# The delta-rule walk emitted in half steps, each tied to its place on TensorE

## The chip, the cores and the metric

The kernel runs on one core of one Trainium2 chip. The metric is the device time of one execution in microseconds; 2858.76 us is the median of three runs of the kernel before. A profile was taken of one further execution.

## The reference, cut to what matters

Two layers of a decoder, each with four mixers side by side on one input projection: HGRN2 (A), gated delta rule (B), Mamba-2 SSD (C), retention (D). The prompt has 2048 positions behind 16 learned ones, so 2064 rows of width 1024; eight sample sequences of one token come along. Each mixer has four heads of 64 x 64 state. The change concerns the gated delta rule, which passes a state S from chunk to chunk:

```
def chunk_gated_delta(S, xs):
    ...
    sol = lax.linalg.triangular_solve(lhs, rhs, left_side=True, lower=True, unit_diagonal=True)
    u = sol[..., :dv] - jnp.einsum('bhik,bhkv->bhiv', sol[..., dv:], S)
    qk = jnp.einsum('bhik,bhjk->bhij', q, k) * decay
    o = (jnp.einsum('bhik,bhkv->bhiv', q * jnp.exp(G)[..., None], S)
         + jnp.einsum('bhij,bhjv->bhiv', qk, u))
    S_new = (jnp.exp(g_last)[..., None] * S
             + jnp.einsum('bhjk,bhjv->bhkv', k * jnp.exp(g_last - G)[..., None], u))
```

The u of a chunk needs the state, and the state of the next chunk needs u: a chain.

## The kernel before, in words

**Stages.** A layer runs the mixers one after the other: C, then B's dense part and preparation, then A (HGRN), then D (retention), then the output projection. The 2064 rows are 17 tiles: tile 0 with 32 prompt rows (and the 8 samples), tiles 1 to 16 with 128 rows. Tiles are dealt to 8 blocks of two (the first has three). A dense group (`dense_cm`, L484 to L486) is 24 matmuls on one PSUM buffer "pd" of two, with one eviction behind it; `dense_rows` (L494 to L496) is the same by rows.

**The walk.** The delta rule's chain is worked in chunks of 32 tokens, so a tile has 4 steps and tile 0 has one. The chain can't be done in one go without leaving TensorE idle, so it is a Python generator, `walkB`, that runs along with the dense part of B and with A: wherever the code calls `hook()`, the generator is advanced to its next `yield` and emits a piece of the walk there. In B's dense part a hook stands after each dense group (8 a block); in A a block of two tiles has 6 hooks between its dense groups and 9 in its inner part (one after the first score level, a double one after each of two further levels, one after each of two last levels, one after each of two tiles), and the first block has 5 more for tile 0. What is left after D would be emitted in one go before the output projection.

**One step** (`stepB`, L1253 to L1273) does, in this order: two state products on TensorE (`wo<-sbd,bnq`, L236), VectorE's add that makes the step's u (`wz<-bwi,wo`, L1264), a copy of it on GpSimd (`bwi<-wz`, L244), the update product on TensorE (`tr<-wz,bkt`, L236, in a PSUM buffer "tr" of two that all mixers share), ScalarE's decay of the old state (`low`, L306), VectorE's two adds that make the new state (`sbd<-low,tr`, L313), and ScalarE's copy of the step's output rows (`boq<-wo`, L1273). Each fp32 product of two halves shows as four matmuls in the trace. The next step's state products need the new state.

**A tile** begins with `loadB` of the next tile (two loads, `bld<-qkv` and `bld<-bscu`, and two smaller ones, on SP's queue; the second of each group's first tile goes on GpSimd's). After the second to fourth step one of three pieces of `keysB` is emitted, which prepares the next tile (transposes of keys and values L1212 and L1213, decay factors, products with the solved inverse). At its end the 32 x 32 score products (`wo<-bwi,bma`) are written to the walk's own PSUM buffer, the one that held the state products ("wo", one buffer), and VectorE adds them to the output (L1331); then `finish` starts the group normalisation, and its rest (two transposes, two VectorE operations, the store) is emitted after the next tile's first step.

**What sets the order.** The instructions are emitted in the order of the Python code, with priorities in that order (`early()` raises some); a scheduler then orders each engine's queue by priority among those that its own estimate takes to be ready. `inorder((ET.PE,))` ties the TensorE instructions emitted inside it behind the last TensorE instruction emitted before it. Before the change only the pieces of `keysB` in a tile are tied so (KORD is 1), the steps, the scores and `finish` are not. Constants in use: LAG 3 (yields after a first load), KB0 1 (keys from the second step on).

Weights, activations, the walk's loads and other tiles share pools: "f4" has five buffers for weight pieces `wr`, the walk's `bld` and A's and the output projection's rows. The weights of A are loaded while the last blocks of B's dense part run.

## Time and profile before

| | |
|---|---|
| runs of the kernel before | 2858.45, 2858.76, 2864.55 us; median 2858.76 |
| profiled execution, its own time | 2864.64 us |
| its span, first to last instruction | 2862.9 us |
| mean granted TensorE clock | 0.982 of full speed |
| instructions | 66636 |

PE is TensorE's matmuls, PEld its weight loads, DVE VectorE, ACT ScalarE, POOL GpSimd, SP the engine whose queue issues most DMAs. Names such as `wz<-bwi,wo` say which tile is written from which. In a timeline a row is a run of like instructions: start, duration, engine, line, operation, tiles, shapes, count, and in brackets the idle time of the engine before it and what ended it.

### The profile page before, as it was taken

How to read it: one execution, taken by the hardware profiler on the slowest of the kernel's cores; microseconds unless marked ns; L12 is line 12 of the kernel's file. 1: busy time of each engine (PE TensorE's matmuls, PEld its weight loads, DVE VectorE, ACT ScalarE, POOL GpSimd, SP SyncE). 2: the span in 40 equal slices, each digit the busy share in tenths (PEclk: the TensorE clock that was granted, in tenths of full speed). 3: DMA queues.
4: the chain of work that ended last, by engine and by line, in shares of the span. 5: the costliest groups of instructions: out<-in, count | busy, mean ns of one | idle time of the engine just before them, and what ended most of it. 6: DMA issues, size and time to landing. Idle time of an engine off the chain costs nothing.

```text
span 2862.9 us, 66636 instructions
## 1 busy us (share of the span) xinstructions
PE 2713.3 (95%) x26372; PEld 2463.7 (86%) x26372; DVE 1704.0 (60%) x4864; ACT 1034.1 (36%) x2601; POOL 1065.6 (37%) x2032
## 2 busy tenths in 40 slices
PE   6999999989999899999989999999999999999998
PEld 6889898989889788888778999888898887888787
DVE  5777765657656655454346767656676667445533
ACT  4545532333434422232244445223443443222321
POOL 4454545557323221110033535555773322211100
PEclk9999999999999999999999999999999999999999
DMA  7243445563321423236672433544632323331443
GB/s 179 67 142 110 147 128 139 149 173 102 98 74 61 150 77 113 77 112 204 211 231 80 127 108 119 141 121 134 184 82 90 88 83 114 98 108 67 139 140 111
DMA packets 385152, 349.31 MB, mean 122 GB/s; under 512 B 144312, under 2 KB 349616, under 8 KB 374600
## 3 DMA queue, kind: packets, MB, share of 16 engines
q1 hardware_dynamic: 381320, 335.95, 38.8%
q0 software_dynamic: 3520, 9.09, 1.7%
q8 instruction: 209, 3.42, 0.5%
q14 instruction: 103, 0.84, 0.1%
HBM read 247.05 MB, written 98.10 MB: 121 GB/s over the span
## 4 chain that ended last, share of the span: by engine, by line
PE 74%; DVE 8%; DMA 7%; POOL 4%; ACT 3%; issue 3%; SPq 1%; POOLq 0%; ACTq 0%; DVEq 0%
PE pd L494 10%; PE pd L496 9%; PE pd L495 9%; PE pd L484 9%; PE pd L485 8%; PE pd L486 8%; PE tr L236 7%; PE wo L236 4%; PE sc L236 4%; PE o L236 3%; DMA wr<-in_w_in_dram 3%; PE tr L622 1%; ACT wh L458 1%; PE tr L518 1%; POOL bR L1168 1%
## 5 line engine op out<-in xcount | busy, mean ns | idle before, releaser
L484 PE MATMUL pd<-xh,wh 128*128 128x256 f32 (+1 forms) x2816 | 828.4, 294 | 34.7 <-DVE hB L959 11.5
L486 PE MATMUL pd<-xh,wl 128*128 128x256 f32 (+1 forms) x2816 | 814.8, 289 | 0.6 <-DVE wl L459 0.6
L485 PE MATMUL pd<-xl,wh 128*128 128x256 f32 (+1 forms) x2816 | 815.3, 290 | 0.0
L484 PEld LDWEIGHTS pd<-xh,wh 128*128 128x128 f32 x2816 | 542.7, 193 | 56.9 <-issue 20.0
L494 PE MATMUL pd<-wh,xh 128*128 128x512 f32 (+5 forms) x1632 | 563.1, 346 | 7.4 <-DVE sraw L1406 4.4
L495 PE MATMUL pd<-wl,xh 128*128 128x512 f32 (+5 forms) x1632 | 558.2, 342 | 5.1 <-POOL wl L459 4.4
L496 PE MATMUL pd<-wh,xl 128*128 128x512 f32 (+5 forms) x1632 | 558.2, 342 | 0.0
L486 PEld LDWEIGHTS pd<-xh,wl 128*128 128x128 f32 x2816 | 542.8, 193 | 5.2 <-issue 3.2
L485 PEld LDWEIGHTS pd<-xl,wh 128*128 128x128 f32 x2816 | 542.9, 193 | 3.1 <-issue 1.3
L494 PEld LDWEIGHTS pd<-wh,xh 128*128 128x128 f32 (+1 forms) x1632 | 304.1, 186 | 45.7 <-issue 4.6
L495 PEld LDWEIGHTS pd<-wl,xh 128*128 128x128 f32 (+1 forms) x1632 | 304.4, 187 | 41.6 <-POOL wl L459 5.0
L496 PEld LDWEIGHTS pd<-wh,xl 128*128 128x128 f32 (+1 forms) x1632 | 304.0, 186 | 38.6 <-issue 1.7
L313 DVE TENSOR_TENSOR sbd<-low,tr 64x128 f32<-64x128 f32 x384 | 109.0, 284 | 130.0 <-PE tr L236 116.1
L336 POOL TENSOR_TENSOR fm<-fm,expo 128x4 f32<-128x4 f32 (+3 forms) x136 | 131.1, 964 | 80.0 <-DVE fm L613 72.6
L611 POOL TENSOR_SCALAR fm<-fm 128x4 f32<-128x4 f32 (+3 forms) x102 | 25.0, 245 | 352.1 <-DVE fm L608 325.4
L340 POOL TENSOR_SCALAR rm<-rm 128x1 f32<-128x1 f32 (+1 forms) x51 | 14.0, 275 | 353.5 <-ACT junk L358 352.5
L244 POOL COPY bwi<-wz 32x256 f32<-32x256 f32 x128 | 59.8, 467 | 206.7 <-DVE wz L1264 203.7
L531 ACT ACTIVATE th<-pd 128x256 f32<-128x256 f32 (+2 forms) x162 | 62.5, 386 | 187.4 <-PE pd L486 143.5
L1168 POOL TENSOR_TENSOR bR<-bR,bW 128x120 f32<-128x120 f32 (+14 forms) x300 | 119.0, 397 | 21.0
L1167 POOL TENSOR_TENSOR bW<-bU,bR 128x120 f32<-128x120 f32 (+14 forms) x300 | 112.8, 376 | 33.2 <-DMA bR<-bscr 12.8
L1674 DVE TENSOR_TENSOR hx<-hx,pd 128x512 f32<-128x512 f32 (+1 forms) x68 | 46.6, 686 | 119.9 <-PE pd L496 118.5
L513 DVE SCALAR_TENSOR_TENSOR hx<-hx,rm,sq 128x512 f32<-128x512 f32 (+1 forms) x68 | 53.1, 819 | 104.5 <-POOL rm L336 103.5
(531 smaller groups left out, 5135.6 us busy)
## 6 DMA issues: line engine op xcount, KB each, us to landing
xh<-xh SPq DMA_DIRECT2D x56, 1024.0 KB
xl<-xl SPq DMA_DIRECT2D x56, 1024.0 KB
wr<-in_w_in_dram SPq DMA_DIRECT2D x64, 512.0 KB
hx<-in_x_prompt_dram SPq DMA_DIRECT2D x32, 512.0 KB
y<-y SPq DMA_DIRECT2D x128, 128.0 KB
yf<-y SPq DMA_DIRECT2D x32, 512.0 KB
bld<-qkv SPq DMA_DIRECT2D x32, 384.0 KB
xh<-xh SPq DMA_DIRECT2D x8, 1184.0 KB
```

The costliest lines, as they stand in the source:

```text
L236: T.matmul(out, l, r, start=start, stop=stop, skip_group_check=True)
L313: tt(new[rr, :, hh], low[rr, :, hh], pv, ALU.add)
L336: G.tensor_tensor(dst, src, e.broadcast_to(list(src.shape)), ALU.pow)
L484: T.matmul(ps, hi[:, d], b.xh[:, d, 0:b.n], start=(d == 0), stop=False)
L485: T.matmul(ps, hi[:, d], b.xl[:, d, 0:b.n], start=False, stop=False)
L486: T.matmul(ps, lo[:, d], b.xh[:, d, 0:b.n], start=False, stop=(d == 7))
L494: T.matmul(ps[0:R, 0:n], xh[:, d], hi, start=(d == 0), stop=False)
L495: T.matmul(ps[0:R, 0:n], xh[:, d], lo, start=False, stop=False)
L496: T.matmul(ps[0:R, 0:n], xl[:, d], hi, start=False, stop=(d == 7))
L531: act(th[0:R, 0:n], ps, AF.Tanh, scale=0.5)
L1167: f(wv, bcm(U_[0:2 * nu, j, j + 1:32], 1, m), bcl(R_[0:2 * nu, 0:m, j], 31 - j), ALU.mult)
L1168: f(R_[0:2 * nu, 0:m, j + 1:32], R_[0:2 * nu, 0:m, j + 1:32], wv, ALU.subtract)
```

## The change

`stepB` gets a `yield` between the state products (with VectorE's add and the copy) and the update. In `walkB` each half is emitted at a hook of its own, and all that is emitted at a hook is tied on TensorE behind what was emitted before. With each half comes one other piece at most: first the ended tile's remainder (two pieces, the scores with the normalisation, then the transposes and the store), else a load that is missing, else, from the second step on, a piece of the next tile's keys. The scores go to a "tr" buffer. The turn of its own that a tile's end, its rest and each piece of keys had is gone.

```diff
--- before.py
+++ after.py
@@ -1265,6 +1265,7 @@
             gcopy(wt[r], xw_[r])
         else:
             V.tensor_copy(xw_[r], wt[r])
+        yield
         R = 128 if SB is not None else 32
         pu = update(lambda p: X.kt[0:R, 2 * p:2 * p + 2].rearrange("t h k -> t (h k)"), xw_[0:R])
         next_state(L, "B", pu, lambda p: X.eg[:, p, 32 * bb + 31:32 * bb + 32])
@@ -1290,8 +1291,20 @@
             x = next(src, 0)
             return x and loadB(L, *x)
 
-        Z = Y = None
-        last = None
+        def ends(X):
+
+            def scores():
+                pi = ptile(ptr, "tr")
+                blocks32(lambda r, h: pi[r, 64 * h:64 * h + 64], X.ma, X.wi.rearrange("t (h v) -> t h v", h=4), X.Lc, True)
+                if X.t == 0:
+                    V.tensor_copy(L.o0[0:32], pi[0:32, 0:256])
+                    L.z0 = dec_z(X.z)
+                    return None
+                tt(X.oq, X.oq, pi[:, 0:256], ALU.add)
+                return finish(X.t, 1, X.oq, 128, X.P.epsq[:, X.i], L.wB, X.z)
+            return scores
+
+        Z = last = None
         done = 0
         while done < NT:
             X = Z
@@ -1307,32 +1320,25 @@
             X.wo = ptile(pwo, "wo")
             X.oq = bk([128, 256], "boq")
             for bb in range(X.Lc // 32):
-                stepB(L, X, bb)
-                yield
-                if last:
-                    last()
-                    last = None
+                step = stepB(L, X, bb)
+                for half in range(2):
+                    with inorder((ET.PE,)):
+
+                        next(step, 0)
+                        if last:
+                            last = last()
+                        elif not Z:
+                            Z = load()
+                        elif bb >= KB0 or X.t == 0:
+                            if not hasattr(Z, "keys"):
+                                Z.keys = keysB(L, Z)
+                            next(Z.keys, 0)
                     yield
-                if not Z:
-                    Z = load()
-                elif bb >= KB0:
-                    if not hasattr(Z, "keys"):
-                        Z.keys = keysB(L, Z)
-                    with inorder((ET.PE,)) if KORD else ExitStack():
-                        k = next(Z.keys, 0)
-                    if k != 0:
-                        yield
-            pi = X.wo
-            blocks32(lambda r, h: pi[r, 64 * h:64 * h + 64], X.ma, X.wi.rearrange("t (h v) -> t h v", h=4), X.Lc, True)
-            if X.t == 0:
-                V.tensor_copy(L.o0[0:32], pi[0:32, 0:256])
-                L.z0 = dec_z(X.z)
-            else:
-                tt(X.oq, X.oq, pi[:, 0:256], ALU.add)
-                last = finish(X.t, 1, X.oq, 128, X.P.epsq[:, X.i], L.wB, X.z)
+            last = ends(X)
             done += 1
+        while last:
+            last = last()
             yield
-        last()
         store_state(L.S["B"], o["gdn_p"][L.l])
 
     def decB(L, ys, epsq):
```

## Rows read from the trace of the kernel before

**Rows 1.** The page, part 1: busy us (share of the span) and instructions of each engine

```profile
PE 2713.3 (95%) x26372; PEld 2463.7 (86%) x26372; DVE 1704.0 (60%) x4864; ACT 1034.1 (36%) x2601; POOL 1065.6 (37%) x2032
```

**Rows 2.** Busy time by stretch: columns in the first line

```profile
core 0: us, PE busy (x) PEld busy (x) DVE busy (x) ACT busy (x) POOL busy (x), PEclk, DMA share, GB/s
455.00:627.00 172.00, 159.38 (x2009) 151.02 (x1998) 97.59 (x294) 60.49 (x144) 92.96 (x199) 0.96 0.54 154
627.00:1022.00 395.00, 376.65 (x5151) 341.99 (x5149) 264.14 (x861) 156.94 (x430) 162.07 (x391) 0.98 0.31 92
1880.00:2035.00 155.00, 147.87 (x1821) 139.71 (x1822) 91.97 (x278) 54.06 (x135) 83.56 (x177) 0.97 0.51 147
2035.00:2432.00 397.00, 379.62 (x5164) 344.17 (x5163) 267.10 (x860) 159.85 (x432) 170.33 (x408) 0.99 0.33 98
```

**Rows 3.** Timeline, TensorE in the delta-rule stage: start us, duration us, what

```profile
500.34 0.61 PE L236 MATMUL tr<-wz,bkt 128*128 128x128 f32 x4
...
503.75 0.61 PE L236 MATMUL wo<-sbd,bnq 128*128 128x128 f32 x4
```

**Rows 4.** Busy time by stretch, four short stretches, columns as in rows 2

```profile
830.50:842.50 12.00, 7.11 (x38) 5.61 (x34) 6.54 (x20) 5.18 (x16) 4.49 (x8) 0.72 0.35 97
...
633.00:662.00 29.00, 29.00 (x301) 27.37 (x301) 17.61 (x74) 8.29 (x25) 21.29 (x48) 1.00 0.46 124
...
2244.00:2256.00 12.00, 8.36 (x51) 6.77 (x52) 7.31 (x23) 5.28 (x16) 4.19 (x8) 0.72 0.35 95
...
594.00:616.00 22.00, 12.96 (x87) 12.34 (x87) 8.40 (x20) 7.94 (x14) 10.67 (x15) 0.77 0.91 211
```

**Rows 5.** Timeline, TensorE in an HGRN block's inner part; idle time before in brackets

```profile
832.37 0.71 PE L236 MATMUL tr<-wz,bkt 128*128 128x128 f32 x4 [1.15 <-DVE wz L1264]
...
833.92 0.68 PE L236 MATMUL wo<-sbd,bnq 128*128 128x128 f32 x4 [0.38 <-DVE sbd L313]
...
835.77 1.22 PE L236 MATMUL tr<-wz,bkt 128*128 128x128 f32 x4 [1.17 <-DVE wz L1264]
...
839.19 1.19 PE L236 MATMUL wo<-sbd,bnq 128*128 128x128 f32 x4 [1.78 <-DVE sbd L313]
```

**Rows 6.** Waits of TensorE, whole span: total us, times, longest us

```profile
PE tr L236 <- DVE wz L1264: 7.2, 10, 1.2
...
PE wo L236 <- DVE sbd L313: 6.1, 8, 1.8
...
PE tr L1212 <- DMA bld<-qkv: 3.8, 3, 1.8
...
PE tr L236 <- DVE sbd L313: 2.8, 6, 0.7
```

**Rows 7.** Instructions on the tile bwi: ns min/median/max, first and last start us

```profile
L236 PE MATMUL wo<-bwi,bma x1040: 214/214/239, 463.1 to 2428.0; 32*32 32x64 f32 x174
```

**Rows 8.** Busy time on tile wz alone, HGRN stage: PE, PEld, DVE, POOL

```profile
627.00:1022.00 395.00, 34.15 (x200) 27.69 (x200) 20.45 (x49) 23.40 (x49) 0.98 0.31 92
```

**Rows 9.** Waits of TensorE in the HGRN stages, layer 0 and layer 1

```profile
PE sc L236 <- DVE ak L795: 2.2, 1, 2.2
...
PE sc L236 <- ACT sq L841: 2.6, 3, 1.5
```

**Rows 10.** Timeline: a first-of-group load on SP, and its transposes on TensorE

```profile
528.01 1.72 SPq L1188 DMA_DIRECT2D bld<-qkv  x2
...
534.03 0.33 PE L1212 MATMUL tr<-ident,bld 128*128 128x128 f32 x1 [1.81 <-DMA bld<-qkv]
```

**Rows 11.** Timeline of SP and VectorE near 600 us; TensorE's wait behind it

```profile
594.30 4.22 SPq L1190 DMA_DIRECT2D bld<-bscu  x1
...
602.50 6.26 SPq L451 DMA_DIRECT2D wr<-in_w_in_dram  x3
...
599.70 1.22 DVE L459 TENSOR_TENSOR wl<-wr,wh 128x1024 fp32r<-128x1024 f32 x1 [6.35 <-ACT wh L458]
...
PE pd L484 <- DVE hB L959: 6.3, 1, 6.3
```


## Prediction

> **What bounds the kernel now.** I read the page's busy line first, then busy time by stage, then who TensorE waits for, then single stretches of the timeline. TensorE has a matmul in flight for 95% of the span and VectorE works 60% [rows 1]: it is a matmul kernel with 2862.9 - 2713.3 = 149.6 us of matmul idle time. By stage [rows 2]: the delta-rule walk (the chain of 32-token steps) begins in the delta-rule stage and ends in the HGRN stage of each layer. From its first step on, the rest of the delta-rule stage (455 to 627, 1880 to 2035) has 12.6 and 7.1 us of matmul idle time, the HGRN stage (627 to 1022, 2035 to 2432) 18.4 and 17.4. So the change works on 55.5 us of idle time, plus what the granted clock (0.96 to 0.99 there) takes.
>
> Where does the walk itself stop TensorE? Beside dense groups, not at all: an update starts at 500.34 and the next state product at 503.75 [rows 3], 3.41 us apart with a dense group of 24 matmuls between them, and 633 to 662 has 29.00 us of matmuls in 29 us [rows 4]. Here each half of a step already has its dense group. In the inner part of an HGRN block the dense groups run out, and steps stand one behind the other: TensorE waits 1.15 us for the update, 0.38 for the next product, 1.17 for the update, 1.78 for the product [rows 5]. That stretch of 12 us has 7.11 us of matmuls and a granted clock of 0.72, as its twin in layer 1 has (8.36 us, 0.72) [rows 4]. Over the whole span the walk's handoffs cost TensorE 7.2 us (update waiting for VectorE's add) and 6.1 us (product waiting for the new state); 2.8 us go to "tr" work waiting for VectorE's state adds, mostly for one of the two PSUM buffers that they hold [rows 6].
>
> **The change, part by part.** I sum against the profiled execution's own time, 2864.64 us (span 2862.9), which is 5.9 above the median of the runs, 2858.76; the same difference is then applied to the median.
>
> **1. Fewer turns.** A turn is one advance of the walk by a hook. Counting yields, a full tile takes 9 turns now (4 steps, 1 for the last tile's rest, 3 for keys, 1 for the tile's end) and 8 then; a layer's walk 151 now and 139 then (3 after the first load, 3 for its keys, 2, 1, 16 x 8, 2 at the end). The delta-rule stage gives 40 turns (5 blocks of 8), the HGRN stage 125 (20, then 7 x 15). So the walk's emission ends at HGRN turn 111 of 125 now and 99 then: 12/15 of a block, some 40 us earlier at (1022 - 627)/8 = 49 us a block [rows 2]. No operation is added or taken away. VectorE, 264.14 busy of 395 us there, covers the denser walk; were that cover gone, 0.83 more steps a block at about 1 us of VectorE would cost 0.8 us a block, 11 us in 14 blocks. I take 0: the last block gets it back.
>
> **2. Halves apart.** The handoffs cost 7.2 + 6.1 + 2.8 = 16.1 us [rows 6]; they lie in HGRN's inner parts. Of a block's 15 turns, 6 follow dense groups and 9 lie in the inner part; 4 of these 9 come as two double turns, where the two halves (or an update and the next product) still stand together. Ends: 0 (each wait only moves) and -16.1. I take the five ninths that get the block's own work in between: **-8.9**. The clock of the two thin stretches costs (1 - 0.72) x 12 = 3.4 us each [rows 4]; ends 0 and -6.7, and the same share gives **-3.7**.
>
> **3. The tile's end.** The 1040 small score matmuls [rows 7] move behind the next tile's first product and from the walk's own PSUM buffer to the shared pair "tr". The walk then takes 9 "tr" buffers a tile instead of 8. A wait of that kind is 2.8/6 = 0.47 us long; ends 0 and 32 tiles x 0.47 = +15. Most find a buffer free, so I take an eighth of 2.8, **+0.4**. The normalisation behind it (ScalarE, VectorE, GpSimd, then two transposes and the store on SP's queue) moves by one turn with the same instructions: 0, since nothing before the output projection reads the store; SP has it in its order either way.
>
> **4. TensorE's order is tied.** Each half's matmuls now come behind the last matmul emitted before them, in the inner part one of HGRN's own, which may itself wait for VectorE or ScalarE. Until now only the keys were tied so; products, updates, scores and transposes could go ahead and fill such a wait. Queued behind a tied half are the next block's dense groups, which are emitted later and may be scheduled ahead of it. Bounds: nothing if those fill instead; at most, with 200/4 = 50 updates a layer in that stage [rows 8], 2 x 50 x 2 halves x 9/15 = 120 halves of 0.61 us of matmuls [rows 3] = +73. The nearest rows are HGRN's own score waits, 2.2 and 2.6 us [rows 9], small today; I let them double: **+4.8**.
>
> **5. Keys and loads.** The next tile's load is issued as now, at a tile's start, but its keys come after 2 turns instead of 3. This counts only for the first tile of a group, the only one not loaded long before: its load was issued at 528.01 and its transposes waited 1.81 us until 534.03 [rows 10]; both layers 3.8 us [rows 6]. Two turns are 2 x 3.41 = 6.8 us, the landing took about 6: I take 0, ends -3.8 and +6.8 (a turn's 3.41 in each layer). The load's four issues (three on SP, and one on SP or GpSimd's queue) move with the tile's start past SP's weight and activation loads. One such place is costly now: the scheduler put load issues among HGRN's weight loads (4.22 us and then 6.26 us on SP), and a dense group waited 6.3 us for VectorE, which stood behind a late weight [rows 11]; the 22 us around it have 12.96 us of matmuls at a clock of 0.77 [rows 4], so 9.0 + 5.1 = 14 us. Layer 1 has no such stall. I take 0, with -14 and +14 as its ends.
>
> **Sum:** -8.9 - 3.7 + 0.4 + 4.8 = **-7.4 us**: 2857.2 for the profiled execution, **2851.4** for the median (-0.26%). A measurement of this kernel can tell about 0.2%, 5.7 us, from no change.
>
> **The rivals.**
> *Nothing measurable.* Beside dense groups the schedule already has the order that the change writes down [rows 3], and in the inner part a wait only goes from one handoff to another. For: VectorE and TensorE take turns there, whoever is served first. Against: the thin stretches are runs of whole steps, which the change breaks up. 2858.8, give or take 4.
>
> *Slower: the walk no longer fills.* If HGRN's own matmuls wait in the inner part and the tied halves stand behind them, TensorE idles where it did a half. From 12.6/0.61 = 21 of the 120 halves on this eats the gain; at 40 it is +24.4 - 12.6 + 0.4 = +12: 2871. For: when the update waited 1.17 us, TensorE did nothing else [rows 5]. Against: HGRN's own waits are short now, and later dense groups may fill. The Trainium skill (TensorE: Matmul & The Clock Gate, step 1 of Part 2) says that only weight loads are pulled ahead and matmuls stay in program order. That speaks against this change, which fixes more of the order, and the trace agrees at that wait. A weight stall as in part 5 arising in layer 1 as well would end near here too, 2851.4 + 14 = 2865.
>
> *Faster by more.* Weight loads filled 27.37 of 29 us, 94%, at full matmul pace [rows 4]; in the two HGRN stretches they fill 686.2 of 792 us [rows 2], so these would take 686.2/0.944 = 727 us at that pace: a room of 65 us where matmul idle time shows 35.8. If half of the room is the walk's, -32: 2826; if the weight stall alone goes, 2837. For: the thin stretches come at block ends. Against: the small matmuls there never run at dense pace. The Trainium skill (Perfetto Trace Analysis, Identifying the Most-Contended Engine) holds matmul busy time for a bad measure of room and weight-load time for a good one. By that rule the larger room is the real one; no row here settles it.
>
> **How the numbers follow.** Small gain as summed (2844 to 2858): 0.36. Nothing measurable: 0.26. Slower: 0.24. Larger gain: 0.14. Faster by over 0.2% (below 2853.0) takes the larger gain and 0.30 of the small one, 0.44; within, 0.26 + 0.06 = 0.32; slower (above 2864.5) 0.24. Faster and slower cases together hold most of the chance; the likeliest one's own range is 2844 to 2858. The range for 8 in 10, 2834 to 2873, reaches to the stall's -14 on one side and to the +12 rival on the other; it leaves out deeper cases of either kind.
>
> **What would show it.** Part 1: the walk's last step in layer 0 some 40 us earlier than now. Part 2: TensorE's waits for the add and the new state fall from 13.3 to under 8 us, and no 12 us stretch at 0.72 in the HGRN stages. Part 3: "tr" waits on state adds still near 3 us. Part 4: HGRN's score waits near 10 us in both layers together; over 20 means the slower rival. Part 5: first-of-group transposes wait 2 us or less. If idle time between 627 and 1022 doesn't fall, the sum is wrong whatever the time.

## The result, and the profile after

The changed kernel takes **2896.13 us** (median of four runs, 2892.57 to 2913.57), the kernel before 2858.61 beside it: a ratio of **1.0142** (95% interval 1.0118 to 1.0166). It is slower by 1.4%, where -0.26% was forecast; the range of 2834 to 2873 missed it by 23 us. The profiled execution took 2898.79 us with a span of 2897.1, so 34.2 us more than the span of before. One execution of the run below with GpSimd tied took 6029.27 us, about twice the others, for no reason that the record shows; without it that run's median is 0.2 us lower.

The page of the changed kernel, part 1:

```profile
PE 2729.6 (94%) x26372; PEld 2474.9 (85%) x26372; DVE 1702.2 (59%) x4864; ACT 1033.9 (36%) x2601; POOL 1053.6 (36%) x2032
```

Every engine has as many instructions as in [rows 1]. Matmul idle time is 2897.1 - 2729.6 = 167.5 us, 17.9 more than before, and the same 26372 matmuls are in flight 16.3 us longer, at a mean granted clock of 0.978 instead of 0.982. So about half of the loss is waiting and half is matmuls that take longer, and no line of the page says where.

To place it, I marked points of equal TensorE work in both traces (each matmul counted by its usual spacing) and compared the time between them. The busy time of the changed kernel by stretch; columns as in [rows 2], whose stretch of layer 0's HGRN stage comes first; then the stretches between points of equal work, and three short ones:

```profile
627.00:1022.00 395.00, 366.90 (x4965) 330.82 (x4964) 249.37 (x824) 152.70 (x418) 155.82 (x386) 0.96 0.32 92
...
617.00:1033.50 416.50, 388.19 (x5176) 349.09 (x5175) 263.98 (x870) 161.20 (x434) 165.56 (x408) 0.96 0.32 94
...
1033.50:1922.60 889.10, 856.32 (x6589) 774.74 (x6588) 502.49 (x1312) 303.90 (x744) 291.59 (x466) 0.99 0.45 135
1922.60:2054.90 132.30, 117.48 (x1413) 112.40 (x1412) 75.72 (x225) 41.48 (x101) 59.84 (x117) 0.94 0.56 155
2054.90:2464.60 409.70, 382.81 (x5185) 345.51 (x5185) 262.79 (x862) 161.06 (x435) 164.25 (x407) 0.97 0.31 92
2464.60:2897.10 432.50, 423.22 (x2550) 362.98 (x2548) 189.33 (x418) 102.28 (x211) 63.24 (x120) 1.00 0.33 109
...
594.00:616.00 22.00, 19.12 (x262) 17.80 (x260) 9.82 (x27) 8.51 (x17) 10.30 (x16) 1.00 1.03 257
850.00:866.00 16.00, 11.99 (x162) 9.58 (x160) 8.53 (x24) 5.61 (x17) 5.95 (x13) 0.79 0.45 129
2026.00:2052.00 26.00, 13.09 (x147) 12.33 (x137) 7.80 (x14) 6.30 (x10) 8.97 (x13) 0.74 0.94 233
```

The same points of work in the kernel before:

```profile
625.00:1014.10 389.10, 370.87 (x5026) 337.13 (x5025) 256.53 (x834) 157.35 (x429) 161.32 (x391) 0.98 0.32 93
...
1014.10:1914.40 900.30, 866.72 (x6738) 781.76 (x6737) 506.15 (x1340) 304.42 (x745) 292.82 (x467) 0.98 0.45 134
1914.40:2033.90 119.50, 112.92 (x1421) 108.17 (x1420) 74.68 (x230) 43.13 (x107) 60.39 (x118) 0.99 0.57 159
2033.90:2423.40 389.50, 372.12 (x5025) 337.68 (x5025) 259.93 (x832) 158.67 (x430) 168.61 (x404) 0.99 0.34 100
2423.40:2862.90 439.50, 427.52 (x2711) 366.00 (x2709) 198.63 (x450) 103.45 (x215) 66.36 (x124) 1.00 0.33 108
```

Read the second column of both, length by length. Up to the first point (617 against 625) the changed kernel is 8.0 us ahead; HGRN costs it 416.5 - 389.1 = +27.4; then -11.2 up to layer 1's delta-rule stage, which costs 132.3 - 119.5 = +12.8; HGRN again +20.2; the rest -7.0. The sum is +34.2. HGRN with what follows costs 16.2 in layer 0 and 13.2 in layer 1, **29.4 us together**, and the delta-rule stages -8.0 + 12.8 = 4.8. The walk now ends earlier, which leaves the last HGRN block and the stages behind it less to do; but of the -11.2 and -7.0 only some 4 us each go with that. The tied kernel before of a run below, whose walk has its old number of turns, takes 893 and 436.5 us for the same two stretches, 7 and 3 us less than before.

**In HGRN** it is the stretches that [rows 4] showed, grown in number: by the trace's record of the granted clock, TensorE runs at the lower of its two levels for 34.1 us of layer 0's HGRN stage (13.7 before) and 23.9 of layer 1's (10.2 before), which costs at most half of the difference, 10.2 + 6.8 = 17.0 us, more (the four matmuls of one product take 0.68 us at the higher level and 1.19 at the lower, at 852.77 and 859.90 below). TensorE at one of them in the changed kernel, rows with a wait and the pieces of the walk (idle time before in brackets):

```profile
851.78 0.65 PE L236 MATMUL tr<-bwi,bma 32*32 32x64 f32 x32
852.77 0.68 PE L236 MATMUL wo<-sbd,bnq 128*128 128x128 f32 x4 [0.34 <-DVE sbd L313]
853.95 0.71 PE L236 MATMUL tr<-wz,bkt 128*128 128x128 f32 x4 [0.50 <-DVE wz L1264]
855.51 0.68 PE L236 MATMUL wo<-sbd,bnq 128*128 128x128 f32 x4 [0.84 <-DVE sbd L313]
857.71 0.41 PE L622 MATMUL tr<-ident,on 128*128 128x128 f32 x2 [1.52 <-DVE on L615]
857.96 0.27 PE L1212 MATMUL tr<-ident,bld 128*128 128x128 f32 x1
...
859.90 1.19 PE L236 MATMUL tr<-cst,bgx 128*128 128x128 f32 x4
...
862.01 1.12 PE L236 MATMUL tr<-tb,bke 128*64 128x128 f32 x8
```

Within 12 us stand the last tile's scores (851.78) and its rest (857.71), the next tile's three keys pieces (857.96, 859.90, 862.01), and between them the handoffs of the steps. The rest waits 1.52 us for the normalised rows `on`, whose normalisation began only with those scores 6 us ago. VectorE says why; its rows there:

```profile
856.68 0.42 DVE L1264 TENSOR_TENSOR wz<-bwi,wo 32x256 f32<-32x256 f32 x1 [1.32 <-PE wo L236]
857.14 0.43 DVE L615 TENSOR_TENSOR on<-boq,fm 128x256 f32<-128x256 f32 x1
```

VectorE stood behind the step's add, which waited 1.32 us for TensorE's product, and only then wrote `on`; TensorE, with the rest tied into its order, waited for that. In 850 to 866 TensorE has 11.99 us of matmuls in 16, and the clock granted is 0.79.

**In layer 1's delta-rule stage** it is one wait. SP and TensorE of the changed kernel:

```profile
2026.24 6.25 SPq L1151 DMA_DIRECT2D bscr<-bdc  x4
...
2033.43 0.54 SPq L1188 DMA_DIRECT2D bld<-qkv  x1
...
2027.44 0.38 PE L622 MATMUL tr<-ident,on 128*128 128x128 f32 x2
2037.84 0.45 PE L1212 MATMUL tr<-ident,bld 128*128 128x128 f32 x1 [10.02 <-DMA bld<-qkv]
```

And before, the same load and its transposes:

```profile
2013.70 0.56 SPq L1188 DMA_DIRECT2D bld<-qkv  x1
...
2039.95 0.27 PE L1212 MATMUL tr<-ident,bld 128*128 128x128 f32 x1
```

Before, 26 us lay between the load's issue and the transposes. Now TensorE has done all that stands in front of them at 2027.82, and the load is issued only at 2033.43, behind four issues that take 6.25 us on SP; 4.4 us after its issue the transposes begin. TensorE has waited 10.02 us by then, and 2026 to 2052 has a clock of 0.74. In layer 0 the reverse happened: the weight stall of [rows 11] is gone, and 594 to 616 has 19.12 us of matmuls at full clock where [rows 4] had 12.96 at 0.77.

TensorE's waits over the whole span, to be read against [rows 6], and HGRN's score waits (layer 0, two rows; layer 1, three) against [rows 9]:

```profile
PE tr L1212 <- DMA bld<-qkv: 10.0, 1, 10.0
...
PE wo L236 <- DVE sbd L313: 7.8, 11, 1.2
...
PE tr L622 <- DVE on L615: 7.3, 8, 1.8
...
PE tr L236 <- DVE wz L1264: 6.2, 10, 0.9
...
PE tr L236 <- DVE sbd L313: 3.9, 5, 1.7
...
PE sc L236 <- DVE aT L788: 1.4, 1, 1.4
PE sc L236 <- ACT sq L841: 0.8, 1, 0.8
...
PE sc L236 <- DVE ak L795: 1.6, 1, 1.6
PE sc L236 <- DVE aS L781: 1.5, 1, 1.5
PE sc L236 <- ACT sq L841: 0.8, 1, 0.8
```

The handoffs cost 7.8 + 6.2 + 3.9 = 17.9 us against 16.1; the scores' waits 6.1 us, where 10 were allowed for and over 20 were to mean the slower rival. The wait for `on`, which [rows 6] doesn't show, costs 7.3; before it was

```profile
PE tr L622 <- DVE on L615: 2.0, 3, 0.9
```

L622 is the transposes of every mixer's normalised rows. Over the whole span all their waits together are 9.4 us before and 8.0 now; in the two HGRN stages they went from 1.9 to 6.2 us.

### The profile page after: what moved, and what is told of

It is laid out like the page before. It is cut to its first block, busy times and chain, and to the rows that moved or that the text cites. A ratio compares the mean times of both kernels' runs of the same rounds, so it can differ in the third digit from the quotient of the medians.

```text
span 2897.1 us, 66663 instructions
## 1 busy us (share of the span) xinstructions
PE 2729.6 (94%) x26372; PEld 2474.9 (85%) x26372; DVE 1702.2 (59%) x4864; ACT 1033.9 (36%) x2601; POOL 1053.6 (36%) x2032
## 4 chain that ended last, share of the span: by engine, by line
PE 73%; DVE 10%; DMA 5%; POOL 5%; ACT 3%; issue 3%; SPq 1%; POOLq 0%; DVEq 0%; ACTq 0%
PE pd L495 10%; PE pd L494 9%; PE pd L496 9%; PE pd L484 8%; PE pd L486 8%; PE pd L485 8%; PE tr L236 8%; PE sc L236 3%; PE wo L236 3%; PE o L236 3%; DMA wr<-in_w_in_dram 2%; POOL bR L1168 1%; PE tr L622 1%; POOL bW L1167 1%; DVE sbd L313 1%
## 5 line engine op out<-in xcount | busy, mean ns | idle before, releaser
L484 PE MATMUL pd<-xh,wh 128*128 128x256 f32 (+1 forms) x2816 | 824.7, 293 | 34.2 <-DVE z L532 7.8
L484 PEld LDWEIGHTS pd<-xh,wh 128*128 128x128 f32 x2816 | 541.1, 192 | 55.9 <-issue 14.7
L336 POOL TENSOR_TENSOR fm<-fm,expo 128x4 f32<-128x4 f32 (+3 forms) x136 | 131.4, 966 | 70.3 <-DVE fm L613 47.7
L1168 POOL TENSOR_TENSOR bR<-bR,bW 128x120 f32<-128x120 f32 (+14 forms) x300 | 119.5, 398 | 21.1
L458 ACT CAST wh<-wr 128x1024 fp32r<-128x1024 f32 x80 | 83.1, 1045 | 83.9 <-DMA wr<-in_w_in_dram 52.0
```

What stands on the lines that cost most here:

```text
L336: G.tensor_tensor(dst, src, e.broadcast_to(list(src.shape)), ALU.pow)
L458: S.copy(hv[:, :, c0:c1], r)
L484: T.matmul(ps, hi[:, d], b.xh[:, d, 0:b.n], start=(d == 0), stop=False)
L1168: f(R_[0:2 * nu, 0:m, j + 1:32], R_[0:2 * nu, 0:m, j + 1:32], wv, ALU.subtract)
```

## The experiments

"Before" and "after" are the two kernels; ratios are to the kernel before, run beside each, with a 95% interval.

### Three suspects taken out of the changed kernel one at a time

**The tie** kept around the keys alone, as before:

```diff
-                    with inorder((ET.PE,)):
-                        next(step, 0)
+                    next(step, 0)
...
-                            next(Z.keys, 0)
+                        with inorder((ET.PE,)):
+                            next(Z.keys, 0)
```

> The changed kernel with the tie on TensorE only around the pieces of the keys, as before the change; half steps, scores and rest are free to go ahead. TIE theory (the walk's matmuls stand behind HGRN's own, which wait): the 20 to 27 us lost in each HGRN stage come back, about 2850 to 2860. HALF theory (two turns a step, each with its own wait in the inner part): the loss stays, 2885 to 2900. TR theory (the scores' use of the shared PSUM pair): stays, 2885 to 2900. LOAD theory (keys sooner after their load): the 17 us at the end of layer 1's delta-rule stage stay, whatever the rest does.

2905.02 us, 1.0165 (1.0140 to 1.0190): no gain. The tie doesn't carry the loss.

**The scores** put back into the walk's own buffer and emitted at once at the tile's end:

```diff
-                pi = ptile(ptr, "tr")
+                pi = X.wo
...
-            last = ends(X)
+            with inorder((ET.PE,)):
+                last = ends(X)()
```

> The changed kernel, but a tile's scores and the start of its normalisation are emitted at once at the tile's end, in the walk's own PSUM buffer, as before the change (tied). TR theory: the loss in the HGRN stages shrinks by most of 45 us, about 2850 to 2860. TIE and HALF theories: within 10 us of the changed kernel, 2886 to 2906.

2932.33 us, 1.0257 (1.0224 to 1.0290): 36 us worse than the change itself. Without a turn of their own at a tile's end, the scores in the one buffer "wo" stand, as I read it, between two tiles' products: the product's wait for the new state is 15.7 us here, 7.8 in the change. But the run moves more than the buffer: the scores now come in front of the next tile's first half step instead of behind it, and the rest takes the half turn that they leave, so that it comes in the same turn. What the buffer alone is worth isn't shown.

**The half steps** put together again in the first of their two turns:

```diff
-                        next(step, 0)
+                        if half == 0:
+                            next(step, 0)
+                            next(step, 0)
```

> The changed kernel, but both halves of a step are emitted at the first of its two turns (tied, same eight turns a tile, same place of the other pieces). HALF theory: the HGRN loss goes, about 2850 to 2860. TIE theory: it stays or grows, 2890 to 2910, since the update too is tied. TR theory: stays, 2885 to 2900.

2902.02 us, 1.0158 (1.0135 to 1.0182): no gain either. The HGRN stages are 10 us shorter in all (406 and 410 us against 416.5 and 409.7), and other stages lose it again. The waits of this kernel, the one that grew (7.3 in the change):

```profile
PE tr L622 <- DVE on L615: 18.9, 14, 3.0
```

### The tie alone, in the kernel before

Steps, rests and scores of the kernel before wrapped in `inorder((ET.PE,))`, nothing else:

```diff
-                stepB(L, X, bb)
+                with inorder((ET.PE,)):
+                    stepB(L, X, bb)
```

> The kernel before with its steps, its tile ends and their rest tied on TensorE, whole steps and nine turns as they were. TIE theory: slower by 30 to 50 us, 2890 to 2908. HALF and TR theories: no change, 2853 to 2864.

**2851.14 us, 0.9973 (0.9957 to 0.9989)**, ten runs: a small gain, where part 4 had a loss of 4.8. It is the base for the runs on before below. HGRN takes it 384.5 and 383.7 us (389.1 and 389.5 before); the second of these stretches:

```profile
2030.00:2413.70 383.70, 369.18 (x5026) 336.32 (x5025) 254.76 (x830) 157.61 (x430) 158.59 (x390) 0.99 0.32 96
```

### What stands where: keys, rest and pace

None of the three suspects was it, so the next runs took the turns themselves. **The keys one turn later**, from the second half of the second step on:

```diff
-                        elif bb >= KB0 or X.t == 0:
+                        elif 2 * bb + half > 2 * KB0 or X.t == 0:
```

> The changed kernel with only the keys one turn later, the rest where the change put it. KEYS theory: 2855 to 2870, no wait over 3 us for a load. REST theory: the HGRN loss stays, only the load wait goes: 2875 to 2890. PACE theory: 2880 to 2895.

2881.32 us, 1.0079 (1.0056 to 1.0101): -14.8 against the change. **The same and the last tile's rest one turn later:**

```diff
-                        if last:
+                        if last and 2 * bb + half != 1:
```

> The changed kernel with the ended tile's rest (two transposes, gating, store) one turn later, at the second step's first half instead of the first step's second, and the three pieces of keys one turn later each. REST theory (the transposes come one turn after the normalisation they read, before it is done): their waits on the normalised rows fall from 6 to under 2 us, and most of the loss in the HGRN stages goes: 2855 to 2870. KEYS theory (the next tile's keys come too soon after their load and beside the steps): the same here. PACE theory (eight turns a tile pack the walk too densely): stays, 2885 to 2900. The 10 us wait for a load at the end of layer 1's delta-rule stage should go by KEYS, 17 us with the clock.

2873.83 us, 1.0049 (1.0032 to 1.0065): a further -7.5. The wait for `on` is 11.2 us (12.2 without the move), so what the rest gives isn't to be read from that row alone. **An empty turn at each tile's end**, nothing else, nine turns a tile:

```diff
             last = ends(X)
             done += 1
+            yield
```

> The changed kernel with one empty turn more at each tile's end, so nine turns a tile as before the change; everything else as changed. PACE theory: the HGRN loss goes, 2855 to 2870. REST and KEYS theories: the loss stays, 2885 to 2900.

2879.63 us, 1.0074 (1.0049 to 1.0098): -16.5; the HGRN stages fall by 24.7 us, to 402.7 and 398.8, and the wait for `bld` from 10.0 to 2.8. And **eight turns in the kernel before**, by leaving out the turn at a tile's end:

```diff
             done += 1
-            yield
         last()
```

> The kernel before without the turn of its own at a tile's end: scores, normalisation and the next tile's first step are emitted in one turn, eight turns a tile. PACE theory: slower by 20 to 40 us, 2880 to 2900. REST and KEYS theories: within 8 us of before, 2850 to 2866.

2872.59 us, 1.0053 (1.0029 to 1.0076): +14.0. Two rows of its waits, which are 3.8 and 6.1 us in [rows 6]:

```profile
PE tr L1212 <- DMA bld<-qkv: 16.9, 3, 7.6
PE wo L236 <- DVE sbd L313: 15.7, 13, 6.8
```

The 6.8 us of the second row is the stall of [rows 11] under another name (at 610 us, VectorE stood 6.91 us behind a late weight), so without it the product's wait is 8.9. The larger part is loads: 7.46 us where layer 1's walk begins (1853.29), and 7.63 for the same tile that waits 10.02 in the changed kernel (2023.76). The HGRN stages, 393.1 and 391.9 us, are only 6.4 longer than before.

So one turn fewer a tile, which part 1 had at 0, costs 14 to 16 us by either way round, but not at the same place: in the changed kernel, whose pieces share turns, in HGRN; in the kernel before mostly at late loads. And that run takes away more than a turn: the scores come right in front of the next tile's first step there, and the rest comes one turn sooner after them.

### The three undone together

Keys and rest later and the ninth turn (the diffs above):

> The changed kernel with the last tile's rest and the keys moved to later half turns, as two runs before, and with an empty turn at each tile's end as well, so nine turns a tile. Crowding theory (the loss is the price of walk pieces standing closer together in the HGRN inner part, by pace and by bunching, each on its own): the two gains add, 2873.8 - 16.5 = 2857, HGRN stages near 390 us each, ratio 0.998 to 1.002. Single-cause theory (moving the pieces and slowing the pace take away the same waits, so they don't add): 2868 to 2876, HGRN stages 392 to 396. If something else in the change costs (the half steps, the scores' buffer, the tie of the rest), what is left over before at this point is its price.

**2861.34 us, 1.0013 (1.0002 to 1.0025)**. The gains nearly add: -14.8 - 7.5 - 12.5 = -34.8 of the 37.5, where -39 was expected. The load's wait is 0.2 us, and the HGRN stretches of this kernel, between the same points of work:

```profile
620.50:1016.20 395.70, 376.09 (x5028) 340.79 (x5027) 254.84 (x836) 157.58 (x426) 156.13 (x390) 0.97 0.31 91
...
2030.90:2424.70 393.80, 376.44 (x5027) 340.76 (x5027) 255.28 (x834) 158.25 (x426) 157.11 (x392) 0.97 0.31 93
```

416.5 and 409.7 us have become 395.7 and 393.8. They are still 6.6 and 4.3 over before, at a clock of 0.97.

### The half steps by themselves

**In the kernel before, tied**, nine turns, only the step split; its update goes into the next turn, beside the piece that has that turn:

```diff
-                with inorder((ET.PE,)):
-                    stepB(L, X, bb)
-                yield
+                step = stepB(L, X, bb)
+                with inorder((ET.PE,)):
+                    next(step, 0)
+                yield
+                with inorder((ET.PE,)):
+                    next(step, 0)
```

> The kernel before, tied, nine turns a tile as before, and only the step split: its state products with the add in one turn, its update in the next turn together with the piece that has that turn already (the last tile's rest, or a piece of the keys). Nothing else of the change. If half steps do what they were forecast to do (waits for the add and the new state move beside other work), it is 5 to 12 us faster than the tied kernel before (2851.1): 2839 to 2846, and TensorE's waits for the add fall from 7.2 us to below 4. If half steps are worth nothing, 2848 to 2854. If an update beside a keys piece costs (both are VectorE chains in one turn, where before each had a turn of its own), 2855 to 2865.

2866.57 us, 1.0029 (1.0016 to 1.0042): 15.4 over its base of 2851.14. Waits of this kernel, and then of its base:

```profile
PE tr L236 <- DVE wz L1264: 20.1, 16, 8.5
...
PE tr L1212 <- DMA bld<-qkv: 15.4, 2, 8.3
...
PE wo L236 <- DVE sbd L313: 5.1, 5, 2.0
```

```profile
PE tr L236 <- DVE wz L1264: 15.0, 14, 7.8
...
PE tr L1212 <- DMA bld<-qkv: 5.9, 2, 4.9
...
PE wo L236 <- DVE sbd L313: 1.1, 4, 0.3
```

Leave out the one long wait of 8.5 and 7.8 (near 606 us in both), and the waits for the add rise from 7.2 to 11.6, those for the new state from 1.1 to 5.1: handoffs cost more with half steps, not less. The load's waits rise by 9.5, outside HGRN. The HGRN stages rise by 12.0, from 384.5 and 383.7 to 387.1 and 393.1; the second of them, to be read against that of the tied kernel:

```profile
2035.30:2428.40 393.10, 374.84 (x5028) 338.73 (x5028) 261.81 (x835) 159.78 (x429) 167.79 (x403) 0.98 0.33 98
```

**In the spread version of the changed kernel** (2861.34, above), whole steps in the first of their two turns (the diff of the whole steps above):

> The changed kernel with nine turns a tile and the last tile's rest and the keys moved later, as two runs before the last (2861.3), and with each step emitted whole in the first of its two turns again. If half steps cost something by themselves, as the run that added them alone to the tied kernel before (2866.6 against 2851.1) suggests, this is 8 to 16 us faster than with them: 2846 to 2853. If half steps are neutral once the pieces are spread and that run's loss was the update beside the keys, 2857 to 2866. If half steps do gain as forecast, it is slower: 2867 to 2875.

2855.54 us, 0.9987 (0.9973 to 1.0001): 5.8 less, a little under the 8 named, although a load is waited for 7.0 us here where layer 1's walk begins (0.2 in all with half steps). HGRN takes 389.2 and 392.3 us, 8.0 less than with half steps. So in all three pairs of runs with and without half steps the HGRN stages are 8 to 12 us longer with them; what comes of it in the whole time goes by the loads.

### Keys early, each in a turn of its own

The kernel before, tied, with the keys after the first step instead of the second (pieces at the third, fifth and seventh of nine turns instead of the fourth, sixth and eighth):

```diff
-    LAG, KB0, KORD = 3, 1, 1
+    LAG, KB0, KORD = 3, 0, 1
```

> The kernel before, tied, nine turns a tile, and only the keys start after a tile's first step and its last tile's rest rather than after the second step, each piece still with a turn of its own. Keys theory (pieces of keys placed sooner cost by themselves, since their loads are later in proportion and less cover is left): 2861 to 2868, 10 to 17 us over the tied kernel before. Bunching theory (what costs is that pieces share turns and blocks' inner parts; spread over nine turns of their own their order is of no matter, beside the first tile of a group): 2848 to 2857, with the late load of a group's first tile as the one loss.

2861.23 us, 1.0013 (1.0000 to 1.0026): +10.1 over its base, at the edge of what the keys theory gave. So early keys cost by themselves, without sharing a turn. Their first load isn't waited for (1.0 us). But the wait that grew in the changed kernel is long here too:

```profile
PE tr L622 <- DVE on L615: 12.7, 7, 4.8
```

Most of it is one wait of 4.57 us at 836 and one of 4.83 at 2247, the same place in both layers. (The tied kernel before waits 3.70 and 3.72 us at these two places too, with nothing in the profile that it waits for.) GpSimd's rows at the first of them:

```profile
834.21 0.45 POOL L1206 TENSOR_TENSOR bld<-bld,cst 128x128 f32<-128x128 f32 x1 [6.30 <-DMA bld<-bscu]
834.62 1.01 POOL L336 TENSOR_TENSOR fm<-fm,expo 128x4 f32<-128x4 f32 x1
```

The first operation of a tile's keys (a subtraction, L1206) waits 6.30 us for the tile's second load, and the last tile's normalisation (L336), whose input VectorE had finished 4 us earlier, stands behind it on GpSimd's queue; VectorE's `on` and TensorE's transposes follow. Four runs tried whether that is the price of early keys. In three, the subtraction and the four copies behind it are only **emitted later**, at the end of the second piece:

```diff
-        gtt(X.tc[0:Lc], X.tc[0:Lc], ...)
-        ...
         ps = ptile(ptr, "tr")
...
+        gtt(X.tc[0:Lc], X.tc[0:Lc], ...)
+        ...
         yield
         pn = ptile(ptr, "tr")
```

In the kernel before with early keys:

> The kernel before, tied, keys early in turns of their own (2861.2), with one thing moved: the GpSimd operations at the head of a tile's keys (one subtraction that waits for the tile's second load, four copies) are emitted at the end of the second piece instead. In the kernel without this move, two twin places (836 us and 2247 us) show that subtraction waiting 6.3 us on GpSimd for the load, the last tile's normalisation behind it on the same queue, and TensorE's transposes 4.6 and 4.8 us behind that. GpSimd theory: those two waits go, 9.4 us and some clock, 2848 to 2853. Rival, the early keys cost by their VectorE and TensorE work: 2858 to 2864, and the two places show another releaser.

In the changed kernel:

> The changed kernel with the same move, nothing else. If the keys' price in it (14.8 us, by placing them one turn later) is the GpSimd operation that waits for the second load in front of the normalisation, 2879 to 2886. If it is the crowding of TensorE and VectorE pieces, or the first load's late issue, 2892 to 2900.

In the tied kernel before:

> The kernel before, tied (2851.1), with the same move and the keys at their old place. If the operation is behind a wait there too, 2840 to 2848; since its keys come a turn later, so that most loads have landed, I expect no difference: 2848 to 2855.

2863.24 (1.0013), 2899.78 (1.0143) and 2851.31 us (0.9977): no difference in any. But none of them tells anything of the theory: the scheduler put the subtraction where it was, and GpSimd's 2032 instructions come in the same order as without the edit in all three (in the first, both waits are there, 4.00 and 4.69 us). They are their base kernels run again, and show how well such a median repeats: within 2.0, 3.7 and 0.2 us. The fourth run **ties it on GpSimd**, behind the second piece's copy:

```diff
-        gtt(X.tc[0:Lc], X.tc[0:Lc], ...)
+        with inorder((ET.Pool,)):
+            gtt(X.tc[0:Lc], X.tc[0:Lc], ...)
```

> The kernel before, tied, keys early in turns of their own, with the GpSimd subtraction of a tile's keys tied on GpSimd behind the copy of the second piece. Emitting it later without the tie had not moved it: the scheduler kept it in front of the normalisation's power on GpSimd, and the two waits of TensorE stayed (4.0 and 4.7 us). GpSimd theory: with the operation truly behind, the two waits for the normalised rows in the HGRN stages go, and with them 9 us and a little clock of the 10 that early keys cost: 2849 to 2854. Rival, crowding on TensorE and VectorE: the waits move to another releaser at the same places and the time stays at 2858 to 2864.

2859.09 us, 1.0002 (0.9988 to 1.0016). Both waits went as the theory had it, to 0.75 us each. Two rows of its waits:

```profile
PE tr L1208 <- DMA bld<-qkv: 7.9, 2, 7.3
...
PE tr L622 <- DVE on L615: 4.2, 6, 0.8
```

8.5 us of waits for `on` are gone, and the time fell by 2.1: a load is waited for 7.3 us where layer 1's walk begins; without the tie the loads' waits were 1.0 us in all. So GpSimd's queue is shown to make those two waits, and isn't shown to make the price of early keys. The HGRN stages speak against it: with early keys they take 393.3 and 393.3 us, 18.4 more than the tied kernel before, and with the GpSimd tie still 391.1 and 391.7, 14.6 more. What doubles there, and stays doubled with the tie, is TensorE's wait for the step's add: 7.2 us in the tied kernel, 14.6 with early keys, 14.7 with the tie. That fits the rival named, crowding on TensorE and VectorE; no run took it away by itself.

### More turns than before

**Ten turns** (a second empty turn at each tile's end of the tied kernel before):

> The kernel before, tied, with one more empty turn at each tile's end, so ten turns a tile where it had nine. Pace theory: eight turns cost 14 us over nine; if that slope goes on, ten turns gain again, 2838 to 2848, with less idle and clock loss in the HGRN stages than 14.5 us and a walk that ends in the last HGRN block or a little in retention. If nine turns already have room enough (the price of pace rises only once pieces share a block's bare turns), 2848 to 2854. If what counts is that the walk ends before HGRN does, the last tile is left over for retention and the output projection waits for it: 2856 to 2870.

2850.84 us, 0.9964 (0.9943 to 0.9984), with runs from 2835.51 to 2866.86: no slope beyond nine turns. HGRN falls further, to 382.0 and 379.9 us, but the profiled execution (2866.86, the slowest) waits 11.8 us for `bld`, 5.0 in layer 0's delta-rule stage and 6.8 where layer 1's walk begins. **The tenth turn only from the sixth tile on**, `if done > 5: yield`:

> The kernel before, tied, with a tenth, empty turn at a tile's end only from the sixth ended tile on, about where HGRN begins; the walk still ends inside HGRN (122 of its 125 turns). Reading of the last three runs: ten turns took the HGRN stages from 384.5 and 383.7 us to 382.0 and 379.9, but the delta-rule stages lost some 11 us each to late loads. If that loss came from the tenth turn inside the delta-rule stage, this kernel keeps the gain without it: 2838 to 2847, ratio 0.993 to 0.996. If it is the place of load issues among weight loads, which any shift of turns deals anew, the time is 2848 to 2862, with the late load in one of the two delta-rule stages.

2856.12 us, 0.9993 (0.9980 to 1.0006). HGRN keeps its gain (384.2 and 378.8), and the time is no better, with one wait of 7.7 us for `bld` where layer 1's walk begins: the second theory. No version here is measurably faster than the tied kernel before, 2851.14.

## Why the prediction was wrong, point by point

**The step that failed first is "I take 0" in part 1.** The fact was read rightly: the walk's last add comes at 991.74 instead of 1012.97, 21 us earlier on the clock and 40 against the end of HGRN, which itself came 19 us later. The price was not: one turn fewer costs 14.0 us in the kernel before and 16.5 in the changed one. The bound of 11 us was worked out from VectorE's busy time alone. What is missing when pieces stand closer isn't VectorE's time but distance: each piece is a chain over two or three engines or waits for a load, and the turn between two pieces was what that hid behind. In the changed kernel it shows in HGRN (24.7 us there come back with the ninth turn), in the kernel before mostly at loads (their waits go from 3.8 to 16.9 us). "The last block gets it back" gave some 4 us a layer, against 27.4 and 20.2 lost.

**Part 5 failed in its scope.** "This counts only for the first tile of a group, the only one not loaded long before" was false at the stage's border. Tile 5 of layer 1, not the first of its group, had 26 us from its load's issue to its keys; now the load is issued 5.6 us after TensorE is ready for them, and a 10.02 us wait came of that. The part also priced only the first piece of keys, which moves from the third turn after the tile's start to the second; the other two move by two and three turns, so that the three now stand in turns one behind the other. The ends of -14 and +14 for the place of load issues on SP were about right, and both came true, in different layers: -8.0 in layer 0's delta-rule stage, +12.8 in layer 1's. But the keys cost more than loads: their earlier place costs 10.1 us with turns of their own and 14.8 in the change. In the former HGRN takes 18.4 us longer, with twice the waits for the step's add, and their GpSimd work blocked the normalisation at two places. No part of the sum had either: it counted what is moved on SP's queue, and not what keys take from the steps and on GpSimd's queue.

**Part 3's "moves by one turn with the same instructions: 0"** failed for the rest. Before, two hooks with a whole step between them lay from the start of the normalisation to its transposes; now one hook with half a step does. Such transposes wait 6.2 us in the HGRN stages (1.9 before), and putting the rest one turn later, with the keys already later, gave 7.5, though its waits fell by only 1.0. The move of the scores to "tr", +0.4, came out small as forecast: "tr" waits on state adds went from 2.8 to 3.9 us. The 36 us of the run that undid the move have other changes in them.

**Part 2, the largest term, had the wrong sign.** Its -8.9 needed the waits for the add and the state to fall from 13.3 to under 8 us; they are 14.0. Half steps alone make the HGRN stages longer, by 12.0 us in the tied kernel before, 8.0 in the spread version and 10 in the changed kernel. In the whole time that is 15.4 and 5.8 us in the first two, and nothing clear of noise in the third (2902.02 without them, 2896.13 with them). The text itself had the reason: beside dense groups the order that the change writes down is there already [rows 3]; and in the inner part, as 850 to 866 shows, the half turns that should fill a handoff carried pieces that wait themselves. The -3.7 for the clock went the other way too: 0.98 and 0.99 in HGRN became 0.96 and 0.97 for the changed kernel as a whole. The text had a test that holds whatever the time is, idle time between 627 and 1022: it rose from 18.4 to 28.1 us.

**Part 4 had the wrong sign.** The tie is worth -7.5 us in the kernel before (4.8 lost were forecast), and taking it off the changed kernel gained nothing. HGRN's score waits are 6.1 us, where they were to double from the 4.8 of [rows 9]. The Trainium skill (TensorE: Matmul & The Clock Gate, step 1 of Part 2) says that only weight loads are pulled ahead and matmuls stay in program order; the prediction read that as speaking against the tie. No run here tests what the page says. But the program's order is made by a scheduler ahead of time, by its estimates, and here the order written down was a little better than the one it chose.

**The rivals.** "Slower" came true by its sign and not by its mechanism: no tied half stood long behind HGRN's own waits, and the late load of layer 1 is 12.8 us of the loss at most. No rival had the pieces' distance from each other as its mechanism, though part 1 and part 5 each named a change in it and set it to 0. The sum put parts 1, 3 and 5 at 0 each; each took distance away at a price, the prices nearly add, and undoing the three gives back 34.8 of 37.5 us.

**What stays open.** Why early keys cost 10 us even in turns of their own is narrowed down to HGRN, not settled: what is behind the doubled waits for the add wasn't tried. A load at the start of layer 1's walk is waited for 7 to 8 us in several of the runs and not in others, and the edits don't touch that place. Runs of the ten-turn kernel spread over 31 us; the profiled one shows late loads, the fast ones have no trace here. And two schedules differ by a few us in stages that the walk doesn't touch (the tied kernel is 7 us faster between HGRN of layer 0 and the delta rule of layer 1), so a single difference of that size can't be put down to the edit alone, and of the 14.0 us of a turn in the kernel before 7.46 is such a load. What HGRN gave back, 24.7 us with the ninth turn, and the 35 us of the three together are far beyond it.

## What to carry to other kernels

When hand-placed pieces of a dependent chain are packed into fewer slots, cost the distance between a piece and the one it depends on (in time at the thinnest place, not in instructions), and never write 0 because the instruction count is the same: here three such zeros were 35 us. Give a piece that ends in a wait of TensorE (transposes behind a normalisation, a product behind a load) a slot at least as far from its producer as it had, and look at stage borders for loads whose lead was only slack of the old pace. Before splitting a step to separate its halves, look whether the scheduler has already separated them, and tie the order first, alone: that was the one part of the change that gained, 0.27% in the kernel before.

## What the runs showed of the hardware that was not expected

Four DMA issues of 64 KB each on SP took 6.25 us (from 2026.24; in the kernel before, the same four took 0.92 and 1.15 us in two pairs at 2008.09 and 2012.50). The load queued behind them was issued 5.6 us after TensorE was ready for it, and the stage lost 12.8 us in a kernel whose TensorE is busy 94% of the time.
